# An encoder kernel whose first projection walks both halves of its columns through fourteen chunks instead of six

## The chip, the cores and the metric

The kernel runs on one core of a Trainium2 chip. The metric is the device time of one execution in microseconds (us). The time before is 2833.39 us, the median of three runs (2833.18 to 2834.37).

## The reference, cut to what matters

The reference is a two-layer encoder over 256 tokens of width 2048, in float32. Each layer does

```python
h = rmsnorm(x, g_mix[i])
z = h @ w_in[i]
dq, dk, dv, cq, ckv, kr, ga, gb = jnp.split(z, split_at, axis=-1)
```

and then two kinds of attention, a gated merge, a SwiGLU block and a gated per-layer embedding. The part that matters here is the very first product of layer 0: `dv`, the 1024 value columns of the differential attention, made from all 2048 input features. Beside it stand the row sums of squares that `rmsnorm` needs, the cosine and sine tables of the two rotary encodings (dimensions 16 and 64), and the two scalars `lam`, which are made from exponentials of dot products of 64 numbers.

## The kernel before, in words

**Layout.** `x` is held transposed in `xT`: 16 chunks of 128 features by 256 tokens. Products run in float32 split into two parts, high and low. `split` makes from a chunk of `x` a tile `ua[j]` whose left 256 columns are the high part (a ScalarE copy) and whose right 256 columns are the low part (VectorE: value times gain minus high). `piece` does the same for a weight: a DMA on SyncE's queue fills a `w32` buffer (1024 float32 a partition), ScalarE copies it to `whi`, VectorE writes the rest to `wlo`. There are four `w32` buffers (`W_BUFS`) and three each of `whi` and `wlo`. A transfer into a `w32` buffer waits on SyncE's queue until both readers of its last contents are done, and every transfer behind it on that queue waits with it.

**The values.** `values` makes the 1024 value columns in two halves of 512. For each of the 16 chunks of features and each half there are six matmuls into two PSUM banks (token blocks `b`): high by high (L464), low by high (L465), high by low (L466). The four banks of the two halves are all four buffers of the pool `ps_mm`, from which the products that follow take theirs too; so the first of them waits until ScalarE has copied the first value bank out (L471). In layer 0 `x` arrives with the values (`load`, L482). The order in which the halves and chunks are walked is written out in `order`: before, six chunks (`BOTH = 6`) make both halves, one `piece` of 512 columns each, then the ten others make half 0 alone (512 columns a piece, `x` in pairs of chunks), then the ten make half 1 alone with pieces of 1024 columns. Each piece takes a whole `w32` buffer, whether it fills it or not.

**The rest of the start.** After half 0, `chores` lets the squares of `x` follow the next four weight pieces (`squared`, ScalarE's Square and VectorE's add). Three small transfers (`small_loads`: rotary constants `rc`, positions, the vectors `lam_in`) follow the first piece of half 1. When half 1 is nearly done come the row norm `R`, `column`, the rotary tables (`tables`) and `lambdas`. `with after_splits()` ties what it holds behind the last piece's split.

**What sets the order.** The programmer's order is not the order on the engines: the framework orders the instructions of each engine by a timeline of its own, and the dependencies become semaphores. On each engine the order is then fixed, and an instruction that waits holds those behind it. Eight matmuls on ones (L480) start TensorE ahead of the first weight.

Of the kernel before, what the change touches and what calls it, by code (L numbers as in the profile page):

```python
# [12 lines left out]
F32 = mybir.dt.float32  # L13
F32R = mybir.dt.float32r
I32 = mybir.dt.int32
AF = mybir.ActivationFunctionType
ALU = mybir.AluOpType
AX = mybir.AxisListType

P = 128  # L20
T = 256
DM = 2048
NC = DM // P
# [13 lines left out]
PT = 8  # L37
W_BUFS = 4
WARM = 8
BOTH = 6  # L40
PAD = 96 - 64 - 8
STEP = 48
FIRST = 7
# [11 lines left out]
def encoder(ctx, tc, x, p, positions, cols, lams, wq, wk, wv, wcq, wckv, wkr, wga, wgb,  # L55
            w_q_up, w_kn, w_v, w_bd, w_bm, w_out, w_gate, w_up, w_down, w_pin, w_pg, rope_c, out):
    nc = tc.nc
    V, A, PE = nc.vector, nc.scalar, nc.tensor
# [6 lines left out]
    ps_mm = pool("ps_mm", 4, space=PSUM)  # L65
# [6 lines left out]
    def bank(ps=ps_at, tag="at", name="at", shape=(P, 2 * T)):  # L72
        return ps.tile(list(shape), F32, tag=tag, name=name)

    def tt(o, a, b, op):
        return V.tensor_tensor(out=o, in0=a, in1=b, op=op)  # L76

    def stt(o, a, s, b, op0, op1):
        return V.scalar_tensor_tensor(out=o, in0=a, scalar=s, in1=b, op0=op0, op1=op1)

    def ts(o, a, s1, s2, op0, op1=ALU.bypass):
        return V.tensor_scalar(out=o, in0=a, scalar1=s1, scalar2=s2, op0=op0, op1=op1)  # L82
# [20 lines left out]
    at = 0  # L103
# [18 lines left out]
    posi = aside[0][:, 0, :].bitcast(I32)  # L122
    posf = aside[0][:, 1, :]

    def tables():
        V.tensor_copy(posf, posi)
        got = []
        for i, name in enumerate("pm"):
            ang, k, r, a = (aside[j + i][:, m, :] for j in (1, 3) for m in range(2))
            ts(ang, posf, rc[:, 2 * i : 2 * i + 1], None, ALU.mult)  # L130
            ts(k, ang, 1.0 / TWO_PI, ROUND, ALU.mult, ALU.add)
            ts(k, k, ROUND, None, ALU.subtract)
            stt(r, k, -C1, ang, ALU.mult, ALU.add)
            stt(r, k, -C2, r, ALU.mult, ALU.add)
            stt(r, k, -C3, r, ALU.mult, ALU.add)
            ts(r, r, PI_IN, -PI_IN, ALU.min, ALU.max)
            stt(a, r, -1.0, r, ALU.mult, ALU.min)
            ts(a, a, math.pi / 2, None, ALU.add)
            cs = const.tile([P, T], F32, name="cos_" + name)
            sn = const.tile([P, T], F32, name="sin_" + name)  # L140
            A.activation(cs, a, AF.Sin)
            A.activation(sn, r, AF.Sin)
            ts(sn, sn, rc[:, 2 * i + 1 : 2 * i + 2], None, ALU.mult)
            got += [cs, sn]
        return got

    neg_lam = const.tile([P, DEPTH], F32, name="neg_lam")
    gsub = const.tile([P, DEPTH], F32, name="gsub")
# [3 lines left out]
    def small_loads():  # L152

        for o, i in (
            (rc, rope_c),
            (posi, positions.to_broadcast([P, T])),
            (lam_in, lams.to_broadcast([P, DEPTH * 256]).rearrange("p (l f d) -> p l f d", l=DEPTH, f=4)),
        ):
            tc.keep_in_program_order(nc.sync.dma_start(o, i))
# [14 lines left out]
    def piece(src, n, high=0, low=0):  # L174


        w = wts.tile([P, PT * P], F32, tag="w32", name="w32", bufs=W_BUFS)
        lo = wts.tile([P, PT * P + 64], F32R, tag="wlo", name="wlo", bufs=3)[:, low : low + PT * P]
        if not step:
            step.append(wts.tile([P, STEP], F32, tag="step", name="step", bufs=1))  # L180
            nc.gpsimd.memset(step[0], 0.0)
        hi = wts.tile([P, PT * P + 64], F32R, tag="whi", name="whi", bufs=3)[:, high : high + PT * P]
        m = n * P
        dst = w[:, :m]
        if len(src.shape) == 3:
            dst = dst.rearrange("p (a b) -> p a b", a=src.shape[1])
        nc.sync.dma_start(dst, src)
        last_split[:] = A.activation(hi[:, :m], w[:, :m], AF.Copy), tt(lo[:, :m], w[:, :m], hi[:, :m].bitcast(F32), ALU.subtract)  # L188
        if chores:
            with after_splits():  # L190
                chores.pop(0)()
        return hi, lo

    def squared(c):
        for j in range(c // 2, c // 2 + 2):
            sq0.append(fb(j))
            A.activation(sq0[j], xT[:, 2 * j : 2 * j + 2, :], AF.Square)
            if j:
                tt(sq0[0], sq0[0], sq0[j], ALU.add)

    last_split, last_mm, chores, sq0, step = [], [], [], [], []

    def after_splits():

        stack = ExitStack()
        for i in last_split:
            stack.enter_context(tc.issue_after(i.ins))
        return stack
# [75 lines left out]
    def in_parts(sums):  # L284

        u = stat.tile([P, 2 * T], F32R, tag="sums", name="sums", bufs=1)
        split(u, sums)
        return u

    def row_norm(u):  # L290

        s = bank()
        for j in range(2):
            PE.matmul(s[:, :T], ones_r, u[:, j * T : (j + 1) * T], start=j == 0, stop=j == 1)
        v, a = (scratch("sh", 2) for _ in range(2))
        y = stat.tile([P, T], F32, tag="row", name="row", bufs=2)
        ts(v, s[:, :T], 1.0 / DM, EPS, ALU.mult, ALU.add)
        ts(y.bitcast(I32), v.bitcast(I32), -0.5, 1597463007.0, ALU.mult, ALU.add)
        for _ in range(3):
            stt(a, y, -0.5, y, ALU.mult, ALU.mult)  # L300
            tt(a, a, v, ALU.mult)
            stt(y, a, 1.5, y, ALU.add, ALU.mult)
        return y
# [141 lines left out]
    def values(src, us, load=None):  # L445

        vals = stat.tile([P, 2, 2, 512], F32, tag="vals", name="vals", bufs=1)
        n = len(us)
        order = [(half, a, 2) for half in range(2) for a in range(0, n, 2)]
        if load:  # L450
            order = [(half, a, 1) for a in range(BOTH) for half in range(2)] + [(0, a, 1) for a in range(BOTH, n)] + [(1, a, 2) for a in range(BOTH, n, 2)]
        banks = {}
        for half, a, m in order:
            if a == 0:
                banks[half] = [bank(ps_mm, "mm", "mmv") for _ in range(2)]
            if load and not half and (a < BOTH or a % 2 == 0):
                load(a, 1 if a < BOTH else 2)
            hi, lo = piece(src[half][:, a * 512 : (a + m) * 512], 4 * m, 32, 16)
            for j in range(m):
                s = slice(j * 512, (j + 1) * 512)  # L460
                for b in range(2):
                    xh = us[a + j][:, b * P : (b + 1) * P]
                    xl = us[a + j][:, T + b * P : T + (b + 1) * P]
                    PE.matmul(banks[half][b], xh, hi[:, s], start=a + j == 0, stop=False)  # L464
                    PE.matmul(banks[half][b], xl, hi[:, s], start=False, stop=False)  # L465
                    last_mm[:] = [PE.matmul(banks[half][b], xh, lo[:, s], start=False, stop=a + j == n - 1)]  # L466
            if half or a + m < n:
                yield
            if a + m == n:
                for b in range(2):  # L470
                    A.activation(vals[:, b, half, :], banks[half][b], AF.Copy)  # L471
                if not half:
                    yield vals
# [8 lines left out]
    def load(c, m):  # L482
        tc.keep_in_program_order(nc.sync.dma_start(xT[:, c : c + m, :], x[:, c : c + m, :]))
        for j in range(c, c + m):
            split(ua[j], xT[:, j, :], g("g_mix0", j))

    for L in range(DEPTH):

        steps = values(wv[L], ua, None if L else load)
        for vd in steps:  # L490
            if L == 0 and vd is not None:
                chores.extend(lambda c=c: squared(c) for c in range(0, NC, 4))
                next(steps)
                small_loads()
                for _ in range(3):
                    next(steps)
                with after_splits():
                    tt(sq0[0][:, 0, :], sq0[0][:, 0, :], sq0[0][:, 1, :], ALU.add)
                    parts_ = in_parts(sq0[0][:, 0, :])
                    R = row_norm(parts_)  # L500
                    next(steps)
                    rcol = column(R)
                    cos_p, sin_p, cos_m, sin_m = tables()
                    lambdas()
                break
            if L:
                parts_ = in_parts(acc)
                next(steps)
                R = row_norm(parts_)
                next(steps)  # L510
                rcol = column(R)
                break
        for v in steps:
            vd = vd if v is None else v
# [227 lines left out]
        for part, (f0, f1) in enumerate(FF_PARTS):  # L742
            for f in range(f0, f1):
                a = pre.pop(0) if pre else joined(product(w_gate[L, f], ub))
                tt(a, a, R, ALU.mult)
                s = scratch("sig", 2)
# [30 lines left out]
        for n in range(NC - 2 * final):  # L777
            a = pre.pop(0) if pre else joined(product(w_pg[L, n], ub))
            tt(a, a, R, ALU.mult)
            s = scratch("sig", 2)  # L780
# [211 lines left out]
```

## Time and profile before

| | |
|---|---|
| time of three runs | 2833.18, 2833.39, 2834.37 us |
| the profiled execution's own time | 2834.78 us |
| its span (first to last instruction) | 2832.9 us |
| busy share of the span | TensorE 100%, VectorE 73%, ScalarE 54% |
| first value matmul, first matmul behind the values' last | 4.71 us, 53.39 us |
| value matmuls of layer 0 | 192 |

The page calls a matmul busy until its modelled end, and successive matmuls overlap: a value matmul is listed with 0.39 us, but the next one starts 0.23 us after it. So time that TensorE loses is read from the distance between starts and from the count of matmuls in a stretch, not from its busy share alone. "Idle before" in brackets is time in which the engine did nothing ahead of a row, with what ended it. SPq is SyncE's queue, on which the transfers are issued one behind the other.

### The profile page before, as it was taken

The page shows a single profiled execution, that of the slowest core. Times are in us where ns is not written, and L with a number is a line of the kernel's source. Part 1 is how long each engine was busy: PE and PEld are TensorE (multiplying, and loading weights), DVE is VectorE, ACT ScalarE, POOL GpSimd, SP SyncE. Part 2 cuts the span into 40 slices and gives each one's busy share as a digit, 9 for nine tenths or more (in the row PEclk, how much of TensorE's full clock was granted, in tenths as well). Part 3 has the DMA queues.
Part 4 walks back from the last instruction along what each step waited for, and adds up shares of the span by engine and source line. Part 5 has one row for each costly group of instructions (what it writes and reads, how often), then busy time and mean ns, then how long its engine had stood idle before and what let it go on. Part 6 is the DMA issues. An engine that isn't in the chain of part 4 may idle for free.

```text
span 2832.9 us, 44066 instructions
## 1 busy us (share of the span) xinstructions
PE 2823.3 (100%) x16723; PEld 2493.1 (88%) x16723; DVE 2076.7 (73%) x3562; ACT 1528.8 (54%) x2553; POOL 1.9 (0%) x15
## 2 busy tenths in 40 slices
PE   9999999999999999999999999999999999999998
PEld 7888988888888888888888889888888888888888
DVE  7997668776666766677869976687766667666777
ACT  6676546554444444455646755465544444444556
POOL 0000000000000000000000000000000000000000
PEclk9999999999999999999999999999999999999999
DMA  7545456556665566566665454555566656655664
GB/s 237 172 161 171 158 180 197 194 193 193 188 199 194 183 198 201 194 193 192 194 192 172 156 172 156 187 197 193 193 193 190 197 194 186 202 193 194 193 194 155
DMA packets 157316, 531.36 MB, mean 188 GB/s; under 512 B 17072, under 2 KB 24240, under 8 KB 157104
## 3 DMA queue, kind: packets, MB, share of 16 engines
q1 hardware_dynamic: 156672, 527.96, 58.1%
q8 instruction: 131, 2.15, 0.3%
q14 instruction: 81, 0.66, 0.1%
q10 hardware_dynamic: 432, 0.59, 0.1%
HBM read 526.39 MB, written 2.10 MB: 187 GB/s over the span
## 4 chain that ended last, share of the span: by engine, by line
PE 99%; DMA 1%; DVE 0%; ACT 0%; issue 0%; SPq 0%; DVEq 0%; ACTq 0%
PE mm L213 61%; PE mm L217 31%; PE S L409 1%; PE mmv L464 1%; PE mmv L466 1%; PE mmv L465 1%; PE at L427 1%; PE at L651 1%; DMA xT<-in_x 0%; PE at L706 0%; PE mm L797 0%; PE mm L395 0%; DMA w<-in_wv 0%; DVE wlo L76 0%; PE at L480 0%; PE at L666 0%
## 5 line engine op out<-in xcount | busy, mean ns | idle before, releaser
L188 ACT ACTIVATE whi<-w 128x1024 fp32r<-128x1024 f32 (+2 forms) x1035 | 1063.7, 1028 | 1222.1 <-issue 602.5
L76 DVE TENSOR_TENSOR wlo<-w,whi 128x1024 fp32r<-128x1024 f32 (+2 forms) x1035 | 1225.2, 1184 | 645.9 <-ACT whi L188 637.4
L213 PE MATMUL mm<-ub,whi 128*128 128x512 f32 x3936 | 1340.7, 390 | 0.0
L213 PE MATMUL mm<-ua,whi 128*128 128x512 f32 x3712 | 1274.3, 391 | 0.0
L217 PE MATMUL mm<-ub,wlo 128*128 128x256 f32 x3936 | 1086.2, 277 | 0.0
L217 PE MATMUL mm<-ua,wlo 128*128 128x256 f32 x3712 | 1028.3, 277 | 0.0
L213 PEld LDWEIGHTS mm<-ub,whi 128*128 128x128 f32 x3936 | 737.8, 188 | 152.6
L213 PEld LDWEIGHTS mm<-ua,whi 128*128 128x128 f32 x3712 | 696.1, 188 | 142.1
L217 PEld LDWEIGHTS mm<-ub,wlo 128*128 128x128 f32 x3936 | 739.4, 188 | 1.1
L217 PEld LDWEIGHTS mm<-ua,wlo 128*128 128x128 f32 x3712 | 697.6, 188 | 1.9 <-DVE wlo L76 0.2
L76 DVE TENSOR_TENSOR a<-mm,join 128x256 f32<-128x256 f32 (+1 forms) x423 | 175.0, 417 | 1.6 <-ACT join L826 1.4
L243 ACT ACTIVATE join<-mm 128x256 f32<-128x256 f32 x452 | 165.0, 366 | 5.3 <-PE mm L217 5.0
L76 DVE TENSOR_TENSOR xT<-xT,mm 128x256 f32<-128x256 f32 x256 | 106.9, 420 | 41.3 <-PE mm L217 37.4
L76 DVE TENSOR_TENSOR a<-a,row 128x256 f32<-128x256 f32 (+1 forms) x209 | 87.8, 423 | 5.9
L76 DVE TENSOR_TENSOR a<-a 128x256 f32<-128x256 f32 x120 | 50.9, 426 | 4.0
L464 PE MATMUL mmv<-whi,ua 128*128 128x512 f32 x128 | 51.0, 402 | 1.2 <-ACT whi L188 1.2
L418 ACT ACTIVATE E<-S,nm 128x256 f32<-128x256 f32 x96 | 44.2, 471 | 13.6 <-DVE nm L82 13.6
L76 DVE TENSOR_TENSOR ua<-a,ua 128x256 fp32r<-128x256 f32 x120 | 50.0, 418 | 1.0 <-ACT ua L251 1.0
L465 PE MATMUL mmv<-whi,ua 128*128 128x512 f32 x128 | 50.0, 394 | 0.0
L251 ACT ACTIVATE ua<-a 128x256 fp32r<-128x256 f32 x120 | 48.1, 402 | 2.6 <-DVE a L76 2.6
L466 PE MATMUL mmv<-wlo,ua 128*128 128x512 f32 x128 | 43.1, 395 | 0.1
L76 DVE TENSOR_TENSOR ssq<-ssq,sq 128x256 f32<-128x256 f32 x96 | 40.2, 419 | 0.3 <-ACT sq L281 0.3
(204 smaller groups left out, 1211.4 us busy)
## 6 DMA issues: line engine op xcount, KB each, us to landing
w<-in_w_gate SPq DMA_DIRECT2D x176, 512.0 KB, 4.6
w<-in_w_up SPq DMA_DIRECT2D x176, 512.0 KB, 4.6
w<-in_w_down SPq DMA_DIRECT2D x128, 512.0 KB, 4.3
w<-in_wga SPq DMA_DIRECT2D x64, 512.0 KB, 3.8
w<-in_wgb SPq DMA_DIRECT2D x64, 512.0 KB, 3.9
w<-in_w_out SPq DMA_DIRECT2D x64, 512.0 KB, 4.4
w<-in_w_pg SPq DMA_DIRECT2D x64, 512.0 KB, 4.7
w<-in_w_down SPq DMA_DIRECT2D x64, 384.0 KB, 3.7
```

The source lines that it names most:

```text
L76: return V.tensor_tensor(out=o, in0=a, in1=b, op=op)
L188: last_split[:] = A.activation(hi[:, :m], w[:, :m], AF.Copy), tt(lo[:, :m], w[:, :m], hi[:, :m].bitcast(F32), ALU.subtract)
L213: lead = PE.matmul(acc, hi[:, s], u, start=start, stop=False)
L217: rest = PE.matmul(acc[:, T:], lo[:, s], u[:, :T], start=False, stop=stop)
L243: A.activation(t, acc[:, T:], AF.Copy)
L251: return A.activation(hi, src, AF.Copy), tt(lo, src, hi.bitcast(F32), ALU.subtract)
L409: PE.matmul(S[:, b, :], q[:, b * P : (b + 1) * P], k, start=j == 0, stop=j == len(pairs) - 1)
L418: last_exp[0] = A.activation(E[:, b, :], S[:, b, :], AF.Exp, bias=nm[:, b : b + 1], scale=scale, accum_out=sm[:, b : b + 1])
L427: PE.transpose(tp[:, kb, b * P : (b + 1) * P], W[:, b, kb * P : (kb + 1) * P], ident)
L464: PE.matmul(banks[half][b], xh, hi[:, s], start=a + j == 0, stop=False)
L465: PE.matmul(banks[half][b], xl, hi[:, s], start=False, stop=False)
L466: last_mm[:] = [PE.matmul(banks[half][b], xh, lo[:, s], start=False, stop=a + j == n - 1)]
```

## The change

`BOTH` becomes 14. Each of the first 14 chunks takes one `piece` with two sources: the two halves' 512 columns go into the two halves of one `w32` buffer by two transfers, are split in two steps each on ScalarE and VectorE, and share one `whi` and one `wlo` buffer. The last two chunks come as one piece of 1024 columns for each half. `x` comes chunk by chunk for 14 chunks and as one pair at the end. The three small transfers stand behind chunk 3's weights. The squares follow chunks 3, 7, 11 and the end of half 0. `tables` becomes a generator of four steps (angle and range reduction, then sine and cosine, for each of the two tables) that follow chunks 5, 6, 8 and 9 in the program.

```diff
-BOTH = 6
+BOTH = 14
...
+    got = []
+
     def tables():
         V.tensor_copy(posf, posi)
-        got = []
...
             stt(r, k, -C3, r, ALU.mult, ALU.add)
+            yield
             ts(r, r, PI_IN, -PI_IN, ALU.min, ALU.max)
...
-            got += [cs, sn]
-        return got
+            got.extend([cs, sn])
+            yield
...
-        m = n * P
-        dst = w[:, :m]
...
-        nc.sync.dma_start(dst, src)
-        last_split[:] = A.activation(hi[:, :m], w[:, :m], AF.Copy), tt(lo[:, :m], w[:, :m], hi[:, :m].bitcast(F32), ALU.subtract)
+        srcs = src if isinstance(src, list) else [src]
+        m = n * P // len(srcs)
+        for k, src in enumerate(srcs):
+            dst = w[:, k * m : (k + 1) * m]
...
+            nc.sync.dma_start(dst, src)
+        for k in range(len(srcs)):
+            s = slice(k * m, (k + 1) * m)
+            last_split[:] = A.activation(hi[:, s], w[:, s], AF.Copy), tt(lo[:, s], w[:, s], hi[:, s].bitcast(F32), ALU.subtract)
...
-            order = [(half, a, 1) for a in range(BOTH) for half in range(2)] + [(0, a, 1) for a in range(BOTH, n)] + [(1, a, 2) for a in range(BOTH, n, 2)]
+            order = [(None, a, 1) for a in range(BOTH)] + [(half, BOTH, n - BOTH) for half in range(2)]
...
+            if half is None:
+                hi, lo = piece([src[k][:, a * 512 : (a + 1) * 512] for k in range(2)], 8, 32, 16)
+            else:
+                hi, lo = piece(src[half][:, a * 512 : (a + m) * 512], 4 * m, 32, 16)
+            for j in range(2 if half is None else m):
+                k, c = (j, a) if half is None else (half, a + j)
...
+    making, chunk = tables(), [0]
...
-                chores.extend(lambda c=c: squared(c) for c in range(0, NC, 4))
-                next(steps)
-                small_loads()
-                for _ in range(3):
-                    next(steps)
+            if L == 0:
+                at = chunk[0]
+                chunk[0] += 1
+                if at == 3:
+                    small_loads()
+                if at < BOTH:
+                    with after_splits():
+                        if at % 4 == 3:
+                            squared(at - 3)
+                        elif at > 4:
+                            next(making, None)
+                    continue
                 with after_splits():
+                    squared(NC - 4)
...
-                    cos_p, sin_p, cos_m, sin_m = tables()
+                    for _ in making:
+                        pass
                     lambdas()
+                cos_p, sin_p, cos_m, sin_m = got
```

What the engines get, at the three places that matter. First SyncE's queue from chunk 3 to chunk 5 (`in_wv` is the value weight, `in_x` the input). Before:

```order
L483 DMA xT<-in_x 128x256
L187 DMA w_240<-in_wv 128x512
L187 DMA w_252<-in_wv 128x512
L483 DMA xT<-in_x 128x256
L187 DMA w_267<-in_wv 128x512
L187 DMA w_279<-in_wv 128x512
```

and with the change:

```order
L494 DMA xT<-in_x 128x256
L191 DMA w_231<-in_wv 128x512 x2
L161 DMA rc<-in_rope_c 128x132
L161 DMA fa_126<-in_positions 128x256
L161 DMA lam_in<-in_lams 128x512
L494 DMA xT<-in_x 128x256
L191 DMA w_263<-in_wv 128x512 x2
```

Two transfers now go into one buffer (one name, x2), and the three small transfers stand ahead of chunk 4's `x` instead of behind half 1's first piece.

Second, VectorE around chunks 7 and 8 (`fa` are the tiles of the rotary tables, `fb` those of the squares, `ua` the low part of `x`). Before:

```order
L79 SCALAR_TENSOR_TENSOR ua_82<-xT,gcol,ua_82 128x256
L79 SCALAR_TENSOR_TENSOR ua_83<-xT,gcol,ua_83 128x256
L76 TENSOR_TENSOR wlo<-w_306,whi 128x512
L76 TENSOR_TENSOR wlo<-w_323,whi 128x512
L79 SCALAR_TENSOR_TENSOR ua_84<-xT,gcol,ua_84 128x256
L79 SCALAR_TENSOR_TENSOR ua_85<-xT,gcol,ua_85 128x256
```

and with the change:

```order
L79 SCALAR_TENSOR_TENSOR ua_83<-xT,gcol,ua_83 128x256
L82 TENSOR_SCALAR fa_127<-fa_127 128x256
L76 TENSOR_TENSOR wlo<-w_350,whi 128x512
L79 SCALAR_TENSOR_TENSOR fa_129<-fa_127 128x256
L76 TENSOR_TENSOR wlo<-w_350,whi 128x512
L76 TENSOR_TENSOR fb_255<-fb_255,fb_371 128x512
L79 SCALAR_TENSOR_TENSOR fa_129<-fa_127,fa_129 128x256
L79 SCALAR_TENSOR_TENSOR ua_84<-xT,gcol,ua_84 128x256
L76 TENSOR_TENSOR wlo<-w_380,whi 128x512
L76 TENSOR_TENSOR fb_255<-fb_255,fb_374 128x512
```

The steps of the tables and the adds of the squares now stand between the splits of the chunks.

Third, ScalarE at the end of the values (`mmv` are the value banks, `vals` where they are copied, `lam_s` the exponentials, `w_652` and `w_674` the two weights of the first product behind the values). With the change, from half 1's last weight on:

```order
L194 ACTIVATE whi<-w_576 128x1024
L170 ACT_TABLE_LOAD
L170 ACTIVATE lam_s<-lam_s 128x2
L194 ACTIVATE whi<-w_652 128x1024
L170 ACTIVATE lam_s<-lam_s 128x2
L143 ACT_TABLE_LOAD
L143 ACTIVATE cos_m<-fa_130 128x256
L482 ACTIVATE vals<-mmv 128x512
L194 ACTIVATE whi<-w_674 128x1024
L482 ACTIVATE vals<-mmv 128x512
```

Before, half 0's banks were copied out long ahead of that, with half 1 still to come:

```order
L197 ACTIVATE fb_497<-xT 128x512
L197 ACTIVATE fb_500<-xT 128x512
L471 ACTIVATE vals<-mmv 128x512 x2
L188 ACTIVATE whi<-w_515 128x1024
L197 ACTIVATE fb_521<-xT 128x512
```

The first copy of a value bank now stands behind two loads of ScalarE's function table; the whole program has eight such loads instead of six. Past the first product or two behind the values the engines' orders are those of before, but for a handful of rows that change places.

More of the change, by code (lines that the diff above doesn't have):

```diff
@@ L182, in piece @@
         hi = wts.tile([P, PT * P + 64], F32R, tag="whi", name="whi", bufs=3)[:, high : high + PT * P]
-        m = n * P
-        dst = w[:, :m]
[L185 to L188, printed above, removed]
+        srcs = src if isinstance(src, list) else [src]
+        m = n * P // len(srcs)
+        for k, src in enumerate(srcs):
+            dst = w[:, k * m : (k + 1) * m]
+            if len(src.shape) == 3:
+                dst = dst.rearrange("p (a b) -> p a b", a=src.shape[1])
+            nc.sync.dma_start(dst, src)
+        for k in range(len(srcs)):
+            s = slice(k * m, (k + 1) * m)
+            last_split[:] = A.activation(hi[:, s], w[:, s], AF.Copy), tt(lo[:, s], w[:, s], hi[:, s].bitcast(F32), ALU.subtract)
         if chores:
@@ L454, in values @@
             if a == 0:
[L455 to L459, printed above, removed]
+                for k in (0, 1) if half is None else (half,):
+                    banks[k] = [bank(ps_mm, "mm", "mmv") for _ in range(2)]
+            if load and not half:
+                load(a, m)
+            if half is None:
[4 more added lines that the diff above has]
+                k, c = (j, a) if half is None else (half, a + j)
                 s = slice(j * 512, (j + 1) * 512)
                 for b in range(2):
[L462 to L466, printed above, removed]
+                    xh = us[c][:, b * P : (b + 1) * P]
+                    xl = us[c][:, T + b * P : T + (b + 1) * P]
+                    PE.matmul(banks[k][b], xh, hi[:, s], start=c == 0, stop=False)
+                    PE.matmul(banks[k][b], xl, hi[:, s], start=False, stop=False)
+                    last_mm[:] = [PE.matmul(banks[k][b], xh, lo[:, s], start=False, stop=c == n - 1)]
             if half or a + m < n:
@@ L490, in encoder @@
         for vd in steps:
-            if L == 0 and vd is not None:
-                chores.extend(lambda c=c: squared(c) for c in range(0, NC, 4))
-                next(steps)
-                small_loads()
-                for _ in range(3):
-                    next(steps)
+            if L == 0:
[10 more added lines that the diff above has]
+                    continue
                 with after_splits():
+                    squared(NC - 4)
                     tt(sq0[0][:, 0, :], sq0[0][:, 0, :], sq0[0][:, 1, :], ALU.add)
                     parts_ = in_parts(sq0[0][:, 0, :])
+                    next(steps)
                     R = row_norm(parts_)
-                    next(steps)
                     rcol = column(R)
-                    cos_p, sin_p, cos_m, sin_m = tables()
+                    for _ in making:
+                        pass
                     lambdas()
+                cos_p, sin_p, cos_m, sin_m = got
                 break
```

## Prediction, on record before the changed kernel ran

> **What bounds the kernel now.** I read the page's chain that ended last first, to see which engine sets the end.
>
> ```profile
> PE 99%; DMA 1%; DVE 0%; ACT 0%; issue 0%; SPq 0%; DVEq 0%; ACTq 0%
> ```
>
> TensorE carries 99% of the chain. The change takes no matmul away and adds none, so it can only win time in which TensorE stands still, and only where it moves work: from the start to the end of layer 0's values. How much that is, I read from matmul counts in stretches of that stage (rows: stretch, then its length, then each engine's busy time and count, clock, DMA share, GB/s), and from the pitch of matmuls that follow each other, in the chain in order of time.
>
> ```profile
> 4.70:24.00 19.30, 18.94 (x78) 15.08 (x78) 0.00 (x0) 1.00 0.81 254
> 24.00:48.00 24.00, 23.01 (x92) 16.72 (x93) 1.06 (x2) 1.00 0.78 259
> ...
> 7.60 0.92 PE mmv L466 x4
> ```
>
> Four matmuls in 0.92 us: 0.23 us each. 78 of them need 17.94 us and stand in 19.30 us, 1.36 us lost; 92 need 21.16 and stand in 24.00, 2.84 us lost. Behind 48 us nothing of note is lost. The first 1.36 us begin with slow matmuls, as the timeline of TensorE shows (start, duration):
>
> ```profile
> 4.71 0.80 PE L464 MATMUL mmv<-whi,ua 128*128 128x512 f32 x1
> ...
> 6.52 0.39 PE L464 MATMUL mmv<-whi,ua 128*128 128x512 f32 x1
> ...
> 24.60 0.50 PE L464 MATMUL mmv<-whi,ua 128*128 128x512 f32 x1 [0.95 <-ACT whi L188]
> ```
>
> From 4.71 to 6.52 four matmuls start, 1.81 us instead of 0.92: 0.89 us go to the slow first matmuls, which the change leaves as they are. What is left, 1.36 - 0.89 + 2.84 = 3.3 us, are waits for weights from about 23.6 us on. That is all that the change can win: 0.12%, less than the 0.2% that a measurement of this kernel can tell from no change.
>
> **Why TensorE waits there.** The chain in order of time (start, us, what) shows a loop:
>
> ```profile
> 15.00 0.33 SPq L187
> ...
> 15.37 3.39 DMA xT<-in_x
> ...
> 19.70 0.53 ACT whi L188
> ...
> 20.26 0.70 DVE wlo L76
> ...
> 20.98 0.33 SPq L187
> ...
> 21.36 4.71 DMA xT<-in_x
> ...
> 28.27 0.33 SPq L187
> ```
>
> A low part frees a buffer, SyncE issues into it, the `x` transfer behind it lands after 3.4 to 4.7 us, is split, and its weight's low part frees the next buffer. A lap took 5.98 us (15.00 to 20.98) and 7.29 us (20.98 to 28.27). Four buffers hold four pieces of 512 columns, six matmuls each, so a lap brings 4 x 6 x 0.23 = 5.5 us of work. The transfers themselves are not at their limit:
>
> ```profile
> 0.00:5.00 5.00, 3.95 (x17) 3.78 (x18) 0.96 (x3) 2.63 (x4) 1.91 (x15) 1.00 0.59 184
> 5.00:10.00 5.00, 5.00 (x20) 3.93 (x20) 3.60 (x7) 3.46 (x7) 0.00 (x0) 1.00 0.84 256
> 55.00:60.00 5.00, 5.00 (x31) 4.42 (x31) 5.00 (x14) 3.01 (x4) 0.00 (x0) 1.00 0.72 230
> ```
>
> 256 GB/s at a share of 0.84 make about 305 GB/s at full share (an estimate from the second row).
>
> **The change part by part.**
>
> *Two pieces in one buffer, fourteen chunks.* A lap of four buffers now brings eight pieces, 11.0 us of TensorE. What must pass: a chunk is two pieces and one `x`, 640 KiB; at 305 GB/s 2.15 us, so 8.6 us a lap; from the other side, the longest lap of before, 7.29 us, with four more pieces of 256 KiB (0.86 us each) wholly behind it, 10.7 us. Both ends are under 11.0. A chunk occupies TensorE for 12 x 0.23 = 2.76 us and the transfers for 2.15, where before, from chunk 6 on, a piece with half a pair of `x` brought 1.38 us for 1.29 us of transfer. So the loop no longer holds TensorE: -3.3 us. The five pieces of 1024 columns at the end of half 1 become one; the waits beside them, at 38 to 46 us, are in the sum.
>
> *The three small transfers* move ahead of chunk 4's `x` on SyncE's queue.
>
> ```profile
> 9.67 0.42 SPq L483 DMA_DIRECT2D xT<-in_x  x1
> ...
> 32.45 0.42 SPq L159 DMA_DIRECT2D rc<-in_rope_c  x1
> ...
> 33.39 0.43 SPq L159 DMA_DIRECT2D lam_in<-in_lams  x1
> ...
> lam_in<-in_lams SPq DMA_DIRECT2D x1, 256.0 KB, 5.5
> fa<-in_positions SPq DMA_DIRECT2D x1, 128.0 KB, 5.2
> rc<-in_rope_c SPq DMA_DIRECT2D x1, 66.0 KB, 4.7
> ```
>
> They cost three issues of 0.45 us (0.42 and the step to the next), which nothing awaits: chunks 0 to 3 and these are 15 issues from 0.74 us on and end near 7.5 us, and chunk 4's `x` went out at 9.67 before. In the transfers they put 450 KiB ahead of chunk 4, whose last byte is number 5 x 640 + 450 KiB, 3.74 MB. By 5 us 0.92 MB have come (184 GB/s); the rest takes 9.2 us at 305 GB/s and 11.0 at the 256 measured, so it lands at 14.2 to 16.0 us. Splitting it (0.50 for `x`, 0.62 for a weight, on ScalarE) makes 15.3 to 17.1.
>
> ```profile
> L188 ACT ACTIVATE whi<-w 128x512 fp32r<-128x512 f32 x22 | 13.2, 623 | 3.4 <-DMA w<-in_wv 3.3
> ...
> L252 ACT ACTIVATE ua<-xT,gcol 128x256 fp32r<-128x256 f32 x16 | 7.6, 501 | 9.0 <-DMA xT<-in_x 8.3 <-DMA gcol<-in_cols 0.6
> ```
>
> TensorE starts chunk 4 at 4.71 + 0.89 + 48 x 0.23 = 16.6 us and needs its second half, the last byte, four matmuls later, at 17.5: no cost by either end. If the small transfers hold the engines by as much as they land later than a weight (5.5 instead of 3.5 us), it comes 1.6 us late. Cost 0 to 1.6 us; I take 0.2, near the rate of the stage.
>
> *Tables and squares on VectorE.* Its prices, from groups of instructions in the first 56 us and from its timeline at 58 and 64 us:
>
> ```profile
> L76 DVE TENSOR_TENSOR wlo<-w,whi 128x512 fp32r<-128x512 f32 x22 | 14.7, 691 | 2.8 <-ACT whi L188 2.5
> L79 DVE SCALAR_TENSOR_TENSOR ua<-xT,gcol,ua 128x256 fp32r<-128x256 f32 x16 | 7.3, 484 | 10.2 <-ACT ua L252 10.2
> L76 DVE TENSOR_TENSOR fb<-fb,fb 128x512 f32<-128x512 f32 x7 | 4.8, 686 | 0.2
> ...
> 57.90 0.75 DVE L79 SCALAR_TENSOR_TENSOR fa<-fa,fa 128x256 f32<-128x256 f32 x2
> ...
> 63.97 0.42 DVE L79 SCALAR_TENSOR_TENSOR sh<-row 128x256 f32<-128x256 f32 x1
> ```
>
> For chunks 5 to 13, where the tables stand: two splits of weights 1.38, one of `x` 0.48, four adds over nine chunks 0.30, and seventeen of the 21 table steps over nine chunks at 0.37 (half of the 0.75, the dearest kind) 0.70: 2.86 us a chunk against TensorE's 2.76. Instructions overlap by some 0.08 us each in these listings (two steps take 0.75 us together, one alone 0.42), which over the 5.3 instructions of a chunk takes 0.43 off: 2.43. So VectorE gains 0.33 us a chunk or loses 0.10. Over nine chunks the worst is 0.9 us, and three `wlo` buffers let it be ahead by then; cost 0 to 0.9 us, I take 0.3. What leaves 48 to 65 us, where VectorE was full (5.00 of 5.00 at 55 to 60 us), brings nothing: TensorE was not waiting there.
>
> *ScalarE at the end of half 0.* The first copy of a value bank now stands behind two table loads, and the first product behind the values waits for it.
>
> ```profile
> 60.02 0.36 ACT L243 ACTIVATE join<-mm 128x256 f32<-128x256 f32 x1
> 60.40 1.28 ACT L142 ACT_TABLE_LOAD   x1
> 61.69 0.42 ACT L142 ACTIVATE sin_p<-fa 128x256 f32<-128x256 f32 x1
> ...
> 51.41 0.20 ACT L168 ACTIVATE lam_s<-lam_s 128x2 f32<-128x2 f32 x1 [2.09 <-DVE lam_s L167]
> 51.52 1.05 ACT L188 ACTIVATE whi<-w 128x1024 fp32r<-128x1024 f32 x1
> 52.47 0.18 ACT L168 ACTIVATE lam_s<-lam_s 128x2 f32<-128x2 f32 x1
> 52.90 0.60 ACT L471 ACTIVATE vals<-mmv 128x512 f32<-128x512 f32 x1 [0.25 <-PE mmv L466]
> ```
>
> When TensorE is done with chunk 13, `whi` for the next product may be written: 1.05, then 0.18 (exponential), 1.28 (load), 0.42 (cosine), 0.60 (copy) make 3.5 us. TensorE has 22 matmuls left, 5.1 us. The load ahead of it starts when chunk 12 frees its buffer, 2.76 us earlier, and takes 1.05 + 1.28 + 0.20 = 2.5. Both fit, with 1.6 and 0.2 us to spare: cost 0 us. The Trainium skill, "ScalarE: Activation LUTs", section "What ACT_TABLE_LOAD costs", prices a switch at 1283 ns plus a drain of about 1380 ns, and its advice is to group functions by table set, against which this order goes. The trace agrees on the 1.28 us but shows no drain: the load follows the instruction before it by 0.02 us and the next by 0.01. By the page the two loads would cost 2.8 us more and the sum would be 1.0 us worse (below).
>
> **The sum.** -3.3 + 0.2 + 0.3 = -2.8 us. The profiled execution took 2834.78 us (its span 2832.9 and 1.9 around it), so 2832.0 by it; the median of the runs is 1.39 us below that execution, which gives 2830.6 us.
>
> **Rivals.**
>
> *VectorE becomes the pace (slower than before).* In-order VectorE holds a split of weights behind a table step, and the idle time before its splits, 2.8 us over 22 pieces now or 0.13 each, stays. It decides from a chunk price of 2.76 + 3.3/9 = 3.1 us on. At 2.86 plus two such waits and one wait for `x` (10.2 us over 16, 0.64) a chunk takes 3.76: nine chunks lose 9.0 us, with 3.3 won and 0.2 for chunk 4: +5.9, 2839.3 us. With the waits for `x` gone, 3.12 gives +0.1, 2833.5 us. Against it: the waits of before were for late transfers, which VectorE's load does not cause.
>
> *The loop goes on (no gain).* If transfers at the deeper queue land later by as much as they are more (a 512 KiB weight took 5.88 us in the chain where a 256 KiB one has a median of 3.5), the lap stretches to 11.0 us and over, and TensorE waits as before; 2833.4 us. Against it: a share of 0.84 leaves room.
>
> ```profile
> 34.39 5.88 DMA w<-in_wv
> ...
> w<-in_wv SPq DMA_DIRECT2D x22, 256.0 KB, 3.5
> ```
>
> *The value banks come late.* If the first exponential waits for VectorE's sum as in the row at 51.41, 2.09 us, the chain ends 2.09 - 0.2 - 1.6 = 0.3 us behind TensorE: 2830.9 us. With the page's drains, 2 x 1.38 in place of the 2.09, it is 1.0 us: 2831.6 us.
>
> *It stalls nowhere and the start speeds up too.* All of 3.3 + 0.89 us: 2829.2 us. The floor; over 0.2% faster would need 5.7 us, which the stage does not hold.
>
> **Chances.** Forecast (2829.2 to 2831.2, the floor with it) 0.60; value banks late (to 2831.7) 0.08; half or more of the loop's loss stays (to 2833.9, with the scatter of the runs) 0.20; VectorE the pace 0.10, half of it over 0.2% slower; something not in these rows 0.02. The range from the floor, 2829.2, to 2833.9 leaves out VectorE's case and little else. Over 0.2% faster (under 2827.7) is above what can be won: 0.03. Over 0.2% slower (above 2839.1): 0.05. Within: 0.92.
>
> **What would show it.** Right: 192 value matmuls in about 45.6 us behind 4.71 (44.2 at 0.23 each, 0.9 for the slow ones, 0.5 for the two costs), so that the first product starts near 50.3 us instead of 53.4 (the row below is the first matmul behind the last value matmul now); no wait of TensorE for `whi` behind chunk 4; waits on SyncE's queue for buffers longer, since buffers fill ahead. Table loads 1.28 us with nothing idle around. Wrong: idle time before TensorE's L477 that VectorE's split ends (VectorE the pace), or before L475 with ScalarE waiting for `in_x` or `in_wv` (the loop), or before the first L219 with a copy of `vals` ending it (banks). A difference that lies behind 60 us would mean that I looked in the wrong place.
>
> ```profile
> 53.39 0.35 PE L217 MATMUL mm<-ua,wlo 128*128 128x256 f32 x1
> ```

## The result

The changed kernel took 2830.59 us, the median of 22 runs (2830.07 to 2832.17), against 2834.39 us of the kernel before in 22 runs (2833.18 to 2836.15): a ratio of 0.9987 with a 95% interval of 0.9981 to 0.9993. That is 3.8 us less, by 0.13%: within the 0.2% that was called no change, but outside the scatter.

The page of the changed kernel:

```profile
span 2828.3 us, 44055 instructions
PE 2819.7 (100%) x16723; PEld 2493.5 (88%) x16723; DVE 2076.2 (73%) x3565; ACT 1533.1 (54%) x2558; POOL 1.9 (0%) x15
...
PE 99%; DMA 0%; DVE 0%; DVEq 0%; SPq 0%; ACT 0%; issue 0%
```

The same matmuls in a span 4.6 us shorter. Of the two profiled executions, that of before lies 0.4 us above the median of its runs and this one (2830.14 us) 0.45 us below, so 3.8 us of the 4.6 are the change and the rest is which execution was profiled. The value matmuls by stretch (length; TensorE, its weight loads, and ScalarE's copies of the value banks, each with its count; clock, DMA share, GB/s), and then, from TensorE's timeline, the start and the first matmuls behind the values:

```profile
4.70:24.00 19.30, 19.02 (x82) 15.33 (x83) 0.00 (x0) 1.00 1.01 343
24.00:48.00 24.00, 24.00 (x107) 19.69 (x106) 1.03 (x2) 1.00 0.74 244
48.00:60.00 12.00, 1.48 (x7) 0.87 (x5) 1.31 (x3) 1.00 0.58 191
```

```profile
4.69 0.50 PE L475 MATMUL mmv<-whi,ua 128*128 128x512 f32 x1
...
6.16 0.50 PE L475 MATMUL mmv<-whi,ua 128*128 128x512 f32 x1 [0.28 <-ACT whi L194]
...
49.31 0.40 PE L219 MATMUL mm<-ua,whi 128*128 128x512 f32 x1
49.55 0.28 PE L223 MATMUL mm<-ua,wlo 128*128 128x256 f32 x1
```

From 24 to 48 us TensorE now starts 107 value matmuls instead of 92, and it is never idle. The first product begins at 49.31 us; before, its low matmul followed the last value matmul at 53.39 us, with one high matmul done early. Matched matmul by matmul from TensorE's first on, the two traces are 0.25 us apart at the end of chunk 0, 3.85 at the last value matmul, 4.5 at about 86 us, and 4.5 to the end. So there are three parts: 0.25 us at the start, 3.6 us in the values, 0.65 us between 53 and 86 us. These are sizes in two single executions; the medians of the runs are 3.8 us apart, so in a typical run the parts are together some 0.7 us smaller, and no trace shows which of them.

SyncE's queue still waits for buffers. What it waits for on VectorE in the first 50 us, first before, then with the change (total, times, longest):

```profile
SPq L187 <- DVE wlo L76: 24.3, 20, 2.7
SPq L187 <- DVE fa L126: 2.3, 1, 2.3
```

```profile
SPq L191 <- DVE wlo L76: 7.0, 3, 3.0
SPq L191 <- DVE fa L82: 5.4, 3, 2.7
SPq L191 <- DVE sums L76: 2.8, 1, 2.8
```

Each row names the VectorE step that ended the wait, so they belong together: 26.6 us in 21 waits before, and, with four smaller rows, 20.8 us in 13 waits now. So the queue's waits by themselves do not tell why TensorE no longer waits. What a lap of the four buffers brings does; it has doubled, as the issues show:

```profile
9.64 0.80 SPq L191 DMA_DIRECT2D w<-in_wv  x2
...
17.20 0.80 SPq L191 DMA_DIRECT2D w<-in_wv  x2
```

These are the weights of chunk 4 and of chunk 8, four buffers later: a lap of 7.6 us for 11.0 us of TensorE's work. The windows agree, first of before, then with the change (length; busy time of TensorE, its weight loads, VectorE, ScalarE; DMA share and GB/s at the end):

```profile
20.00:30.00 10.00, 9.05 (x39) 6.80 (x38) 6.47 (x13) 5.80 (x13) 0.00 (x0) 1.00 0.78 248
30.00:40.00 10.00, 9.67 (x40) 6.84 (x39) 6.35 (x10) 5.71 (x10) 0.00 (x0) 1.00 0.86 276
```

```profile
10.00:20.00 10.00, 10.00 (x45) 8.21 (x44) 8.27 (x17) 8.23 (x16) 0.00 (x0) 1.00 1.01 330
20.00:30.00 10.00, 10.00 (x45) 8.22 (x44) 10.00 (x24) 8.50 (x15) 0.00 (x0) 1.00 0.93 327
30.00:40.00 10.00, 10.00 (x46) 8.19 (x45) 9.90 (x22) 8.33 (x18) 0.00 (x0) 1.00 0.71 236
```

From 10 to 20 us the transfers run at their limit (share 1.01, 330 GB/s), get ahead, and fall back to what TensorE uses. VectorE is full from 20 to 40 us, and TensorE waits for none of it.

### The profile page after: what moved, and what is told of

It is laid out like the page before. It is cut to its first block, busy times and chain, and to the rows that moved or that the text cites. A ratio compares the mean times of both kernels' runs of the same rounds, so it can differ in the third digit from the quotient of the medians.

```text
span 2828.3 us, 44055 instructions
## 1 busy us (share of the span) xinstructions
PE 2819.7 (100%) x16723; PEld 2493.5 (88%) x16723; DVE 2076.2 (73%) x3565; ACT 1533.1 (54%) x2558; POOL 1.9 (0%) x15
## 4 chain that ended last, share of the span: by engine, by line
PE 99%; DMA 0%; DVE 0%; DVEq 0%; SPq 0%; ACT 0%; issue 0%
PE mm L219 61%; PE mm L223 31%; PE S L415 1%; PE mmv L477 1%; PE mmv L475 1%; PE mmv L476 1%; PE at L433 1%; PE at L672 1%; PE at L727 0%; PE mm L818 0%; PE mm L401 0%; DMA w<-in_wv 0%; PE at L687 0%; PE at L332 0%; PE mm L874 0%; PE at L300 0%
```

## The experiments

Two theories were set against each other. *The loop*: TensorE waited because a lap of transfer, split and release of four buffers brings only four pieces of 512 columns. *The demand*: it waited because half 0 alone with its `x` asks for 285 GB/s, and both halves together for 237, so that the order of the chunks is what counts.

**Fourteen chunks, a buffer for each piece.**

```diff
-                hi, lo = piece([src[k][:, a * 512 : (a + 1) * 512] for k in range(2)], 8, 32, 16)
+                own = [piece(src[k][:, a * 512 : (a + 1) * 512], 4, 32, 16) for k in range(2)]
```

> Fourteen chunks make both halves as in the change, tables and squares in steps as there, but every piece of 512 columns takes a w32, whi and wlo buffer of its own, so that a lap of four buffers brings four pieces. Theory of the loop (the prediction's): a lap takes 6.0 to 7.3 us and brings 5.5 us of TensorE, so the waits come back: the first product starts at 52 us or later, 2833 us or more. Rival, theory of demand: before, TensorE waited because half 0 alone with its x asks for 384 KiB in 1.38 us (285 GB/s) and both halves together for 640 KiB in 2.76 us (237 GB/s); then the order alone is enough: no waits, first product near 49.5 us, 2830.6 us.

2836.67 us, ratio 1.0009 (1.0000 to 1.0018); the first product starts at 56.08 us. The order of the change alone loses 2.3 us against the kernel before, with an interval that just touches 1. The demand theory falls here. That it loses fits the loop: the kernel before fills five buffers, at the end of half 1, and this one only its last two. But ScalarE's chain in it also ran through a table load, so steps between splits could have had a part.

**The same with all steps behind chunk 15.**

```diff
                 if at < BOTH:
-                    with after_splits():
-                        if at % 4 == 3:
-                            squared(at - 3)
-                        elif at > 4:
-                            next(making, None)
                     continue
                 with after_splits():
-                    squared(NC - 4)
+                    for c in range(0, NC, 4):
+                        squared(c)
```

> Fourteen chunks with a buffer for each piece of 512 columns, as in the first experiment, but squares and tables all behind chunk 15, so that no step stands between the splits. If the loop of the buffers alone made the waits of the first experiment: first product still at 52 us or later, 2833 us or more. If the steps on ScalarE and VectorE made them, with a lookahead of only three pieces: first product near 50 us, 2831 us.

2839.59 us, ratio 1.0018 (1.0009 to 1.0027). Without any step between the splits the waits stay; why it is 2.9 us slower still than the first experiment stays open. The issues and the landings of the chain, in order of time, are the loop:

```profile
14.29 0.33 SPq L191
14.67 5.52 DMA xT<-in_x
...
22.00 0.33 SPq L191
22.38 4.13 DMA xT<-in_x
...
28.79 0.33 SPq L191
29.16 3.59 DMA xT<-in_x
```

Laps of 7.7 and 6.8 us for 5.5 us of TensorE. Counts agree: 73 value matmuls from 4.70 to 24 us where the change has 82, and 98 from 24 to 48 where it has 107.

```profile
4.70:24.00 19.30, 17.22 (x73) 13.54 (x74) 0.00 (x0) 1.00 0.82 252
24.00:48.00 24.00, 23.13 (x98) 17.69 (x97) 0.00 (x0) 1.00 0.74 245
```

**The old order with full buffers.** Six chunks with both halves, then half 0 and half 1 alone, tables and squares as before, but 1024 columns in every buffer.

```diff
-            order = [(half, a, 1) for a in range(BOTH) for half in range(2)] + [(0, a, 1) for a in range(BOTH, n)] + [(1, a, 2) for a in range(BOTH, n, 2)]
+            order = [(None, a, 1) for a in range(BOTH)] + [(half, a, 2) for half in range(2) for a in range(BOTH, n, 2)]
```

> Six chunks make both halves as before, then half 0 alone and half 1 alone, with the tables and squares where they were before; but every buffer is filled: the six chunks put their two pieces of 512 columns into one buffer, and the others come as pieces of 1024 columns. Theory of the loop: a lap brings 11 us of TensorE and the waits go: first product near 49.5 us, 2830.6 us. Theory of demand: half 0 alone still asks for 285 GB/s against the 256 to 281 measured there, so that 1.5 to 3 us of waits stay: first product at 51 to 53 us, 2832 to 2834 us.

2831.18 us, ratio 0.9989 (0.9980 to 0.9998).

```profile
24.00:48.00 24.00, 24.00 (x107) 19.68 (x106) 1.19 (x2) 1.00 0.70 230
...
49.77 0.40 PE L217 MATMUL mm<-ua,whi 128*128 128x512 f32 x1
```

With `BOTH = 6` and the tables in their old place the 3.6 us of the values are there. Half 0 alone no longer waits once its buffers are full: the rate it asks for was there all along. Behind the values this trace gains nothing on that of before; the experiment with the matmuls on ones, below, shows why.

**Which buffer.** A chunk's two pieces share only `w32`, or only `whi` and `wlo`.

```diff
-                hi, lo = piece([src[k][:, a * 512 : (a + 1) * 512] for k in range(2)], 8, 32, 16)
+                own = [piece(src[0][:, a * 512 : (a + 1) * 512], 4, 32, 16)]
+                own.append(piece(src[1][:, a * 512 : (a + 1) * 512], 4, 32, 16, (kept[0], None), 1))
```

(For the second kernel the argument is `(None, kept[1])`: the first piece's `whi` and `wlo`, a `w32` of its own.)

> The change, but only the w32 buffer is shared by a chunk's two pieces; each piece has a whi and a wlo buffer of its own (three of each, so one and a half chunks). If the transfers' buffers set the lap (theory of the loop): few or no waits, first product by 50 us, 2830.6 to 2831.5 us. If the splits' buffers and their lookahead do: waits as in the first experiment, 2833 us or more.

> The change, but only whi and wlo are shared by a chunk's two pieces; each piece has a w32 buffer of its own, so four buffers hold four pieces. Theory of the loop: waits as in the first experiment, first product at 52 us or later, 2833 us or more. If the splits' lookahead is what counts: no waits, 2830.6 us.

Sharing `w32` alone: 2830.68 us, 0.9987 (0.9978 to 0.9996), as the change. Sharing only the split's buffers: 2834.05 us, 0.9998 (0.9990 to 1.0007), as before. First `w32` shared, then `whi` and `wlo`:

```profile
24.00:48.00 24.00, 24.00 (x106) 19.69 (x106) 0.91 (x2) 1.00 0.69 221
...
49.48 0.39 PE L227 MATMUL mm<-ua,whi 128*128 128x512 f32 x1
```

```profile
24.00:48.00 24.00, 23.58 (x102) 18.42 (x101) 0.00 (x0) 1.00 0.80 248
...
52.42 0.39 PE L227 MATMUL mm<-ua,whi 128*128 128x512 f32 x1
```

So one part of the change is enough for the gain in the values: two transfers into one transfer buffer. The split's buffers are not without effect: sharing them alone is 2.6 us faster than the first experiment, where nothing is shared, but it stays 3.4 us behind the change. More buffers of half the content were not run.

**Squares and tables late, all else as in the change** (the diff of the second experiment, on the change).

> The change, with the squares and the tables moved back behind half 0's last piece (all after chunk 15), so that VectorE has only splits during the chunks. If the steps cost nothing where the change puts them and gain nothing where they leave: 2830.6 us, first product near 49.3 us. If they were what delayed VectorE (0.3 us in the prediction): 0.3 us less. Rival: relief of VectorE at 50 to 80 us is worth the 0.65 us that the traces differ behind the values: then 0.6 us more, with a matmul pair at 350 instead of 340 ns between 55 and 75 us.

2831.05 us, 0.9988 (0.9979 to 0.9996). Moving them back gains nothing, so where the change puts them they cost nothing; the medians are 0.5 us to the other side, about the scatter of a kernel's single runs. Behind the values its trace gains 0.5 us on that of before, nearly as the change's does, with the tables back on VectorE there and VectorE busy all of the time from 48 to 60 us. The relief of VectorE is not what gave the 0.65 us.

**More work for VectorE.**

```diff
+            for _ in range(MORE):
+                ts(ang, posf, rc[:, 2 * i : 2 * i + 1], None, ALU.mult)
...
+                stt(r, k, -C3, r, ALU.mult, ALU.add)
             yield
```

> The change, with six steps of each table done three times instead of once: 24 more VectorE instructions during chunks 5 to 13. By the prices of the prediction they add 24 x 0.28 = 6.7 us there, 0.75 a chunk, so that VectorE needs 3.2 us (2.43 + 0.75) to 3.6 us a chunk against TensorE's 2.76. If VectorE is as near to being the pace as the prediction said: waits of 1 to 6 us for wlo, 2832 to 2836 us. If it has room to spare, because the three wlo buffers and the light last chunks take it up: under 0.5 us of waits, 2830.6 us.

(`MORE` is 2.) 2831.16 us, 0.9988 (0.9979 to 0.9997); no wait for `wlo` in the values.

```profile
20.00:30.00 10.00, 10.00 (x46) 8.19 (x45) 10.00 (x25) 8.24 (x17) 0.00 (x0) 1.00 0.92 323
30.00:40.00 10.00, 10.00 (x45) 8.23 (x44) 10.00 (x24) 6.93 (x13) 0.00 (x0) 1.00 0.73 235
40.00:50.00 10.00, 10.00 (x45) 8.19 (x45) 9.88 (x26) 5.89 (x11) 0.00 (x0) 1.00 0.67 207
```

VectorE stays full ten microseconds longer and TensorE keeps 45 matmuls in 10 us. The 24 more instructions do not stretch the chunks: the order on VectorE lets the steps slide to later chunks and keeps the splits ahead of TensorE. Its median is 0.6 us above the change's. In the traces most of that lies behind the values, where this one gains 0.1 us on that of before instead of 0.65.

**The change once more.**

> The changed kernel once more. Behind the values the trace of before had matmul pairs at 350 ns from 58.5 to 78.9 us where that of the change had 340. If that follows from the order of the instructions, this trace shows 340 at 53 to 75 us again, and 350 in the same places elsewhere; if it is chance, the places differ from the first trace of the change. Time 2830.6 us.

2830.44 us, 0.9987 (0.9978 to 0.9995). Value waits worth 3.6 us and the 0.65 us behind them are there again, with 340 ns a pair from 54 us on. The 0.25 us at the start are not: this execution was 0.27 us behind that of before at the end of chunk 0. So the start is chance, and the rest comes back with the order.

**The two matmuls on ones side by side, in the kernel before.**

```diff
-        for j in range(2):
-            PE.matmul(s[:, :T], ones_r, u[:, j * T : (j + 1) * T], start=j == 0, stop=j == 1)
+        for j in (1, 0):
+            PE.matmul(s[:, :T], ones_r, u[:, j * T : (j + 1) * T], start=j == 1, stop=j == 0)
```

> The kernel before, with the two matmuls on ones of layer 0's row norm in the other order (low part first), which puts them next to each other behind a high matmul. In the trace of before the second of them stands alone between a low and a high matmul at 58.5 us, and from there to 78.9 us a pair of matmuls takes 350 ns instead of 340. If the place of that matmul sets the pitch: pairs at 340 from 58 to 79 us and 0.6 us less than before, in this trace against that of before. If VectorE's load there or chance sets it: 350 stays. The values' waits stay as before, first product near 53.4 us; by the comparison 2833.8 to 2834.4 us, too little to tell.

2833.96 us, 0.9998 (0.9990 to 1.0007): as expected too little for the comparison. The traces tell it. TensorE before, ahead of and behind the second matmul on ones and some pairs later:

```profile
58.38 0.28 PE L217 MATMUL mm<-ua,wlo 128*128 128x256 f32 x1
58.50 0.28 PE L294 MATMUL at<-sums,ones 128*128 128x256 f32 x1
58.62 0.39 PE L213 MATMUL mm<-ua,whi 128*128 128x512 f32 x1
...
64.57 0.40 PE L213 MATMUL mm<-ua,whi 128*128 128x512 f32 x1
...
65.97 0.40 PE L213 MATMUL mm<-ua,whi 128*128 128x512 f32 x1
```

and with the two side by side:

```profile
58.24 0.40 PE L213 MATMUL mm<-ua,whi 128*128 128x512 f32 x1
58.47 0.40 PE L294 MATMUL at<-sums,ones 128*128 128x256 f32 x2
58.70 0.28 PE L217 MATMUL mm<-ua,wlo 128*128 128x256 f32 x1
...
64.63 0.39 PE L213 MATMUL mm<-ua,whi 128*128 128x512 f32 x1
...
65.99 0.39 PE L213 MATMUL mm<-ua,whi 128*128 128x512 f32 x1
```

Four pairs take 1.40 us in the first and 1.36 in the second. It holds from 59 to 79 us, and between the last value matmul and 86 us this kernel is 0.6 us faster than before in the matching of the two traces. The other traces fit. In those of full buffers in the old order and of more work for VectorE the second matmul on ones stands alone between a low and a high one too, at 53.69 and 55.28 us, and the pairs take 350 ns from there to 75 us.

**Another start.** Chunk 0's `x` goes out on ScalarE's queue ahead of the gains, so that SyncE's begins with the weight.

```diff
-    nc.scalar.dma_start(gcol, cols)
+    tc.keep_in_program_order(nc.scalar.dma_start(xT[:, 0:1, :], x[:, 0:1, :]))
+    tc.keep_in_program_order(nc.scalar.dma_start(gcol, cols))
```

> The change, with chunk 0's x sent from ScalarE's queue ahead of the gains, so that SyncE's queue begins with the first weight. In the traces so far TensorE's fifth value matmul starts at 6.1 to 6.8 us, when the second half of chunk 0's weight is split, whether the first four run slowly or not. If the issue of that weight is what it waits for: 0.4 us earlier (one issue), fifth matmul near 6.1 us, 2830.2 us. If the rate of the first transfers sets it: no change, 2830.6 us. Worse if the gains, now 0.4 us later, hold the first split.

2831.57 us, 0.9991 (0.9982 to 1.0000): not better than the change, by its median 1 us worse. In its trace the gains come later, the order on ScalarE now has both splits of the weight ahead of that of `x`, and TensorE waits for `x`:

```profile
5.14 0.63 ACT L195 ACTIVATE whi<-w 128x512 fp32r<-128x512 f32 x1 [0.24 <-DMA w<-in_wv]
...
5.68 0.89 ACT L259 ACTIVATE ua<-xT,gcol 128x256 fp32r<-128x256 f32 x2
...
6.23 0.79 PE L476 MATMUL mmv<-whi,ua 128*128 128x512 f32 x1 [1.39 <-ACT ua L259]
...
11.08 0.63 PE L478 MATMUL mmv<-wlo,ua 128*128 128x512 f32 x1
11.51 1.05 PE L476 MATMUL mmv<-whi,ua 128*128 128x512 f32 x2
```

The first of its two theories is not tested by this, since the wait moved to `x`. The profiled execution, 2834.74 us, is the slowest of this kernel; its value matmuls start every 0.43 us until 12.4 us.

## Why the prediction was right, and where it was not

**The time was met by two errors that cancel.** 2830.6 was forecast and 2830.59 measured. That they agree so closely is luck: the forecast gain was 2.8 us and the measured one 3.8; the three runs of before that the sum was set against had a median of 2833.39, and 22 runs have 2834.39.

**What bounds the kernel, and the ceiling of what can be won** held: TensorE is 99% of the chain after as before, and all that moved lies ahead of 86 us. The first product behind the values, forecast near 50.3 us, came at 49.31. The ceiling was set too low. Over what is counted as waits (3.3 us by counts of matmuls, 3.6 by matching the traces) 0.65 us came from a place that the prediction called worthless, "TensorE was not waiting there". It was not waiting, but its matmuls stood 0.005 us further apart, which a count at 0.23 us does not show. Some 0.55 us of it lies behind 60 us, where by the prediction's own sign it had looked in the wrong place.

**The loop** was right in mechanism: the experiments with own and shared buffers show it, and the transfer buffer is the part of it that is enough. The lap was forecast at 8.6 to 10.7 us. The laps that begin from 9.64 to 15.47 us took 7.0 to 7.7: the 8.6 was made from an estimate of 305 GB/s, and full share gave 330 to 343. That SyncE's queue would wait longer for buffers held for each of its waits on VectorE (1.6 us against 1.3), not for their sum (20.8 against 26.6).

**The small transfers ahead of chunk 4**: 0.2 us was taken, 0 was found. The traces of before and after are 0.25 us apart at the end of chunk 0 and 0.25 apart at the start of chunk 4. The last weight of chunk 4 was split on ScalarE at 16.1 us, within the 15.3 to 17.1 of the forecast, and TensorE came to it at 17.3.

**VectorE's steps**: 0.3 us was taken, 0 was found. The price per chunk was about right: from chunk 5's first low part (done at 17.93 us) to chunk 13's (38.47), 2.57 us a chunk, where 2.43 to 2.86 was forecast and TensorE takes 2.75. The prediction named VectorE's lead and still took 0.3: chunk 5's first low part was done 3.0 us before TensorE used it and chunk 13's 4.4 us. It left out that steps can slide to later chunks. The rival that VectorE becomes the pace fell: even 24 more instructions did not bring it.

**The value banks** came in time:

```profile
43.34 1.05 ACT L194 ACTIVATE whi<-w 128x1024 fp32r<-128x1024 f32 x1
44.29 0.19 ACT L170 ACTIVATE lam_s<-lam_s 128x2 f32<-128x2 f32 x1
44.49 1.28 ACT L143 ACT_TABLE_LOAD   x1
45.79 0.42 ACT L143 ACTIVATE cos_m<-fa 128x256 f32<-128x256 f32 x1
46.11 0.58 ACT L482 ACTIVATE vals<-mmv 128x512 f32<-128x512 f32 x1
```

From the split to the end of the copy 3.35 us (3.5 forecast), ended at 46.7 with the product due at 49.31. The load takes 1.28 us and its neighbours stand within 0.02 of it, so a switch of tables costs its own duration here. The Trainium skill, "ScalarE: Activation LUTs", section "What ACT_TABLE_LOAD costs", adds a drain of about 1380 ns; this trace, too, shows none.

**The slow start** was taken as fixed, and it is not: in the profiled execution of the change the first four value matmuls had nearly the full pitch, and TensorE then waited for the second half of chunk 0's weight until 6.16 us, where before four slow ones ended at 6.52. In the repeat it waited until 6.66. In nine of the twelve traces TensorE's fifth weight load waits for that weight, in the trace of before as well, where the slow pace ends at about the same time. In the other three it does not, so neither alone sets the start.

## What to carry to other kernels

When a queue waits for buffers, count the work that one lap of all buffers brings and the time that a lap takes: half-filled buffers halve the first and left the second nearly as it is here (6.0 and 7.3 us half filled, 7.0 to 7.7 full). Filling them can be worth more than the order of the work: here the order alone lost, and full buffers in the old order won all that was to be had in the values. A ceiling for a gain should be made from distances between starts, not from idle time alone, since a busy engine can also run at a slightly longer pitch.

## What the runs showed of the hardware that was not expected

A pair of matmuls of 512 and 256 columns takes 340 ns or 350 (232 and 118 instead of 227 and 113), and it keeps the longer pitch for tens of pairs. In the kernel before this begins where one more matmul of 256 columns stands between a low and a high one, and ends at 79 us where two high ones stand next to each other. The order sets it: two traces of the change agree, and reversing two matmuls in the kernel before takes the longer pitch away. How busy VectorE is does not: with squares and tables late it was busy all of the time from 48 to 60 us and the pairs took 340 ns. Where such a matmul stands close behind another, as in the change, the pitch returned to 340 within four pairs, and where two high ones follow it at once, as with squares and tables late, the pairs stay at 340; by which rule stays open.

In the trace of the last experiment, TensorE's matmuls of 512 columns start every 0.43 us for six microseconds, though the granted clock is listed as 1.00. The Trainium skill, "TensorE: Matmul & The Clock Gate", gives 426.7 ns for a cold matmul of this size in the section "Wait — 56ns, not 53.3ns?", and says in "What's actually happening" that the window that decides runs freely. The trace agrees with the number; why this execution warmed so late, with TensorE idle for 1.4 us behind its warming matmuls, was not tried. Behind the slow matmuls its value matmuls start every 233 ns, where the trace of the change has 229; that, too, stays open.
